# Two more seven-product pairs in the last product's second half, a seventh buffer for arriving weights, residual rows fetched in halves: one Hymba layer in float32

## The chip, the core and the metric

One core of a Trainium2 chip runs the kernel. The metric is the device time of one execution in microseconds. The kernel before was timed in three runs: 1082.09 us in the median, 1081.95 at the lowest, 1083.99 at the highest.

## The reference, cut to what matters

256 tokens with 2048 features pass one layer. All arrays are float32.

```
u    = rmsnorm(h, ln1_w)
proj = u @ W_in                      # six pieces of 1024 columns
y    = [RG-LRU group | retention group]   # 2048 columns
h    = h + y @ w_out                 # 2048 x 2048
u    = rmsnorm(h, ln2_w)
ff   = silu(u @ w_gate) * (u @ w_up) # 5632 columns each
h    = h + ff @ w_down               # 5632 x 2048
out  = rmsnorm(h, final_norm_w)
```

The change lies mostly in `ff @ w_down`, called "down" below, and in buffers that all parts share.

## The kernel before, in words

Each float32 number is cut into a high part (rounded to the format that TensorE multiplies) and the rest, a low part. One product of two blocks then takes three matmuls (`three`: high by high, high by low, low by high). ScalarE makes the high part with a cast and VectorE the low part with a subtraction (`split`, lines 123 and 124; names `wh`, `wl` for a pair of weight blocks, `bh`, `bl` for a single one, `ah`, `al` for a left block, `sh`, `sl` for sums of left blocks).

**Weights.** They arrive in loads of 128 x 1024 numbers (512 KB) from the queue of SyncE (SP) into `raw` buffers, of which there are six, and pass through `split` into `wh` and `wl` buffers, of which there are four pairs. From the fourth multiplication block on (`swap`), two more `raw` buffers (`raw2`) and two more pairs of split buffers (`split2`) exist: every fourth load takes one of the former, every third split one of the latter. Before the last gate/up block, `stop_more` ends their use, and ahead of down `swap_back` gives their memory to the residual rows (`resid2`, eight tiles) and the final norm's weights (`fw`), which GpSimd's queue then loads.

**Pairs.** After the projections every product runs over *pairs*: two 128-row pieces of the left matrix for both token halves (a11, a12, a21, a22) by the four weight blocks of 512 columns that go with them. A plain pair takes eight products. A summed pair takes seven (Strassen-Winograd): VectorE adds up weight blocks (`Quad.add`, line 661, four additions of 128 x 512) and left blocks (s1 to s4), and the sums are split as well. A plain pair needs two wide splits of weights, a summed one a narrow split (b11) and three wide ones.

**Down.** `down_block(d, ...)` runs twice, for d = 0 (output columns 0 to 1023) and d = 1 (1024 to 2047), with 22 pairs each; the texts call them block 0 and block 1. `ORDER_DOWN[d]` lists the order of the pairs, `SUMMED_DOWN[d]` which of them are summed. The left blocks are the same in both (`make_left` keeps them in `dl`). The results p1, p5, p6, p7 of the summed pairs and c11, c12, c21, c22 collect in TensorE's accumulators. When a collected c is complete, VectorE adds it to the residual row tile `htok` (line 941), ScalarE squares that tile for the final norm into a tile called `junk` that nobody reads (line 979, with a running sum), and VectorE multiplies `htok` by the norm's weights `fw` (line 984). For block 0 this work falls into the start of block 1.

**Small tiles.** Everything of 128 x 512 (left blocks, `bh`, `bl`, `part`, `junk`, `sq`) comes from one rotating pool of 60 buffers (`act_tile`). A new tile waits for the last reader of the tile that had its buffer before.

**The start.** `squares` (line 308) squares the eight tiles of x for the first norm. The first square goes to `sumsq`, the other seven to `sq` tiles that GpSimd adds to `sumsq` (lines 310, 311); TensorE then sums over partitions (`rms`, line 271) among the matmuls of the next projection.

A scheduler of the framework decides each engine's order when the kernel is built; the two last pairs of block 1 alone have a fixed order. Every engine works through its own list strictly in that order.

## Time and profile before

| | |
|---|---|
| median of three runs | 1082.09 us (1081.95 to 1083.99) |
| profiled execution | 1082.46 us |
| its span in the trace | 1080.7 us |
| outside the span | 1.8 us |
| TensorE busy (matmul / weight load) | 1070.2 us (99%) / 897.7 us (83%) |
| VectorE busy | 964.1 us (89%) |
| ScalarE busy | 664.5 us (61%) |
| GpSimd busy | 57.2 us (5%) |
| mean granted TensorE clock | 0.998 |

Busy times are sums over one execution. An engine that is off the chain of waits can be idle at no cost; TensorE, which is on it nearly throughout, can't.

### The profile page before, as it was taken

What the parts mean: (1) busy time and instruction counts of PE and PEld (TensorE: products, weight loads), DVE (VectorE), ACT (ScalarE), POOL (GpSimd) and SP (SyncE); (2) the same over time, 40 slices, a digit from 0 to 9 for tenths busy, and PEclk for the clock granted to TensorE, in tenths of its full rate; (3) what the DMA queues carried; (4) which work ended last, traced back from release to release, by engine and by line L of the source; (5) the groups of instructions that cost most, each with busy time, mean ns of one, the idle gap of its engine ahead of it and who ended that gap; (6) DMA issues with size and microseconds to landing.
All of it is one profiled execution on the core that took longest, in us unless ns stands there. A gap on an engine that the chain in (4) does not pass through costs nothing.

```text
span 1080.7 us, 14590 instructions
## 1 busy us (share of the span) xinstructions
PE 1070.2 (99%) x5089; PEld 897.7 (83%) x5089; DVE 964.1 (89%) x1399; ACT 664.5 (61%) x947; POOL 57.2 (5%) x73
## 2 busy tenths in 40 slices
PE   9999999999999999999999999999999999999997
PEld 7888888888888888888888888888888888888886
DVE  7889789988878889989999999999999889997886
ACT  7666644468756676656656565665656656654563
POOL 0602230000000000000000000000002000000001
PEclk9999999999999999999999999999999999999999
DMA  9965475554556588677776777777767856474662
GB/s 325 336 213 171 159 254 166 183 176 158 192 195 234 183 304 273 231 235 256 257 270 228 251 260 242 263 269 232 258 234 270 289 181 214 162 245 159 214 212 101
DMA packets 71386, 244.62 MB, mean 226 GB/s; under 512 B 8208, under 2 KB 8592, under 8 KB 71312
## 3 DMA queue, kind: packets, MB, share of 16 engines
q1 hardware_dynamic: 68400, 236.34, 64.6%
q0 software_dynamic: 1472, 4.72, 1.3%
q10 hardware_dynamic: 1440, 2.62, 0.6%
q8 instruction: 40, 0.66, 0.2%
q14 instruction: 34, 0.28, 0.1%
HBM read 239.46 MB, written 4.19 MB: 225 GB/s over the span
## 4 chain that ended last, share of the span: by engine, by line
PE 98%; DVE 1%; DMA 1%; POOL 0%; SPq 0%; ACT 0%; issue 0%; POOLq 0%; ACTq 0%
PE c L685 22%; PE c L683 22%; PE c L684 22%; PE fm L194 11%; PE fm L196 5%; PE tm L174 3%; PE tm L175 3%; PE tm L176 3%; PE p L683 1%; PE p L685 1%; PE p L684 1%; PE ft L865 1%; DMA x<-in_x 1%; PE ht L588 0%; PE sc L492 0%; DVE wl L124 0%
## 5 line engine op out<-in xcount | busy, mean ns | idle before, releaser
L123 ACT CAST wh<-raw 128x1024 fp32r<-128x1024 f32 (+1 forms) x498 | 462.9, 959 | 323.8 <-PE c L685 130.8
L124 DVE TENSOR_TENSOR wl<-raw,wh 128x1024 fp32r<-128x1024 f32 (+1 forms) x498 | 542.2, 1115 | 72.5 <-ACT wh L123 71.2
L684 PE MATMUL c<-wl,ah 128*128 128x512 f32 x826 | 322.7, 391 | 0.0
L685 PE MATMUL c<-wh,al 128*128 128x512 f32 x826 | 321.8, 390 | 0.0
L683 PE MATMUL c<-wh,ah 128*128 128x512 f32 x826 | 280.3, 391 | 0.0
L683 PEld LDWEIGHTS c<-wh,ah 128*128 128x128 f32 x826 | 155.1, 188 | 32.0 <-ACT wh L123 0.3
L685 PEld LDWEIGHTS c<-wh,al 128*128 128x128 f32 x826 | 155.2, 188 | 31.8
L684 PEld LDWEIGHTS c<-wl,ah 128*128 128x128 f32 x826 | 155.2, 188 | 31.6
L194 PE MATMUL fm<-u,wh 128*128 128x512 f32 x512 | 161.4, 396 | 0.0
L196 PEld LDWEIGHTS fm<-u,wl 128*128 128x128 f32 x512 | 96.1, 188 | 22.4
L196 PE MATMUL fm<-u,wl 128*128 128x256 f32 x512 | 101.2, 279 | 0.0
L661 DVE TENSOR_TENSOR raw<-raw,raw 128x512 f32<-128x512 f32 x114 | 78.4, 689 | 2.0
L661 DVE TENSOR_TENSOR raw<-raw 128x512 f32<-128x512 f32 x114 | 78.3, 688 | 1.4
L194 PEld LDWEIGHTS fm<-u,wh 128*128 128x128 f32 x512 | 78.4, 189 | 0.3
L684 PE MATMUL c<-wl,sh 128*128 128x512 f32 x192 | 74.3, 390 | 0.0
L685 PE MATMUL c<-wh,sl 128*128 128x512 f32 x192 | 73.7, 390 | 0.0
L683 PE MATMUL c<-wh,sh 128*128 128x512 f32 x192 | 67.3, 391 | 0.3 <-ACT sh L123 0.3
L176 PE MATMUL tm<-wh,u 128*128 128x512 f32 x128 | 48.7, 391 | 0.0
L175 PE MATMUL tm<-wl,u 128*128 128x512 f32 x128 | 48.7, 393 | 0.0
L174 PE MATMUL tm<-wh,u 128*128 128x512 f32 x128 | 46.9, 394 | 1.4 <-ACT u L298 1.4
L683 PEld LDWEIGHTS c<-wh,sh 128*128 128x128 f32 x192 | 36.1, 188 | 8.1 <-ACT sh L123 0.7
L685 PEld LDWEIGHTS c<-wh,sl 128*128 128x128 f32 x192 | 36.1, 188 | 7.5
(247 smaller groups left out, 1027.4 us busy)
## 6 DMA issues: line engine op xcount, KB each, us to landing
raw<-in_w_gu SPq DMA_DIRECT2D x216, 512.0 KB, 5.3
raw<-in_w_down SPq DMA_DIRECT2D x91, 512.0 KB, 4.6
raw<-in_w_out SPq DMA_DIRECT2D x34, 512.0 KB, 3.7
raw<-in_w_lx SPq DMA_DIRECT2D x16, 512.0 KB, 6.4
raw<-in_w_k SPq DMA_DIRECT2D x16, 512.0 KB, 3.6
raw<-in_w_q SPq DMA_DIRECT2D x16, 512.0 KB, 4.2
raw<-in_w_rg SPq DMA_DIRECT2D x16, 512.0 KB, 3.5
raw<-in_w_lg SPq DMA_DIRECT2D x16, 512.0 KB, 3.5
```

Of the source, the lines that this page charges most:

```text
L123: act.copy(out=dst_h, in_=src)
L124: v.tensor_tensor(out=dst_l, in0=src, in1=dst_h.bitcast(F32), op=ALU.subtract)
L174: pe.matmul(ps, ah, wh, start=first, stop=False)
L175: pe.matmul(ps, ah, wl, start=False, stop=False)
L176: pe.matmul(ps, al, wh, start=False, stop=last)
L194: pe.matmul(ps, wh, hl, start=n + i == 0, stop=False)
L196: pe.matmul(ps[:, :S], wl, hl[:, :S], start=False, stop=n + i == len(order) - 1)
L661: v.tensor_tensor(out=dst, in0=a, in1=b, op=ALU.add)
L683: pe.matmul(p, ah, bh, start=first, stop=False, skip_group_check=onto)
L684: pe.matmul(p, ah, bl, start=False, stop=False, skip_group_check=onto)
L685: pe.matmul(p, al, bh, start=False, stop=last, skip_group_check=onto)
L865: pe.transpose(pt[:, o : o + P], g[:, (2 * b + c) * P : (2 * b + c) * P + P], ident)
```

## The change

- Block 1 of down has nine summed pairs instead of seven: 12 and 19 are added. They were summed in block 0 already, so their left sums exist; the tiles of these sums now come from a pool of their own (`sums`, four buffers) that is opened in block 0 and closed after the pair in place 7 of block 1. The order of block 1 changes so that plain and summed pairs alternate from its second pair on, with 12 and 19 in front.
- There are seven `raw` buffers all through. The extra `raw2` buffers are taken by kind: by the loads of `Direct` and by the second half of a block's last plain pair. The extra split buffers stay in use until the pair in place 6 of block 0 of down.
- The residual rows come back in two halves: four tiles, then `fw`, from the pair in place 9 of block 0 on, and the other four tiles after the pair in place 7 of block 1.
- `sumsq` and the rotation tables `cr`, `sr` come from the pool of 60 instead of buffers of their own.

```diff
-SUMMED_DOWN = (9, 12, 15, 17, 19), (5, 7, 9, 11, 13, 15, 17)
-ORDER_DOWN = (3, 4, 0, 5, 6, 1, 7, 8, 2) + tuple(range(9, 22)), tuple(range(22))
+SUMMED_DOWN = (9, 12, 15, 17, 19), (5, 7, 9, 11, 12, 13, 15, 17, 19)
+ORDER_DOWN = (3, 4, 0, 5, 6, 1, 7, 8, 2) + tuple(range(9, 22)), (0, 12, 1, 19, 2, 5, 3, 7, 4, 9, 6, 11, 8, 13, 10, 15, 14, 17, 16, 18, 20, 21)
+BESIDE = (12, 19)
...
-    rpool = ctx.enter_context(tc.tile_pool(name="raw", bufs=6))
+    rpool = ctx.enter_context(tc.tile_pool(name="raw", bufs=7))
...
-    def raw_tile():
-        turn_of[0] += 1
-        pool_ = more[0] if more and turn_of[0] % 4 == 0 else rpool
+    def raw_tile(brief=False):
+        pool_ = more[0] if more and brief else rpool
...
-    sumsq = cpool.tile([P, 512], F32, name="sumsq")
+    sumsq = act_tile("sumsq")
...
-    cr = cpool.tile([P, S], F32, name="cr")
-    sr = cpool.tile([P, S], F32, name="sr")
+    turned = act_tile("turned")
+    cr, sr = turned[:, :S], turned[:, S:]
...
+            if i in hooks[ordered]:
+                program.append(([], hooks[ordered][i]))
...
+            place = sum_tile if p in BESIDE else act_tile
+            dl[p] = Left(ff[p], p in EARLY_DOWN + SUMMED_DOWN[0] + SUMMED_DOWN[1], place)
...
+    def rows_back(d):
+        resid[0] = ctx.enter_context(tc.tile_pool(name=f"resid_{d}", bufs=4))
+        for key in [(cb, t) for cb in (2 * d, 2 * d + 1) for t in range(2)]:
+            htok[key] = res_tile("htok")
+            pool.dma_start(out=htok[key], in_=kept[key])
+
     def swap_back():
         extra.close()
+        rows_back(0)
         late.append(ctx.enter_context(tc.tile_pool(name="late", bufs=4)))
-        resid[0] = ctx.enter_context(tc.tile_pool(name="resid2", bufs=8))
-        for key in [(cb, t) for cb in range(4) for t in range(2)]:
-            htok[key] = res_tile("htok")
-            pool.dma_start(out=htok[key], in_=kept[key])
         load_fw()
+        sums_kept.append(beside.enter_context(tc.tile_pool(name="sums", bufs=4)))
+
+    def sums_end():
+        beside.close()
+        rows_back(1)
+
+    hooks = {0: {6: stop_more, 9: swap_back}, 1: {7: sums_end}}
...
-        if b.index == NB + 1:
-            program.append(([], stop_more))
         b.put(after)
-    program.append(([], swap_back))
```

What it does to each engine's list shows in rows of the program, in an engine's order, without times. Numbers at the end of names tell tiles apart; in brackets stands whose progress a row waits for ("DMAHW", "DMASW": a load).

**ScalarE, where block 0 of down ends and block 1 begins, before.** The four squares are the rows of line 979.

```order
L123 CAST wh_1962_9171<-raw_1961_9169 128x1024 [waits DMAHW3_49,DVE_49,PE_49]
L123 CAST wh_1969_9237<-raw_1968_9235 128x1024 [waits DMAHW4_49,DVE_49,PE_49]
L979 ACTIVATE junk_1964_9188,ssq_121<-htok_1735_8244 128x512 [waits DVE_49]
L979 ACTIVATE junk_1965_9203,ssq_121<-htok_1737_8248 128x512 [waits DVE_49,Activation_49]
L979 ACTIVATE junk_1966_9218,ssq_121<-htok_1736_8246 128x512 [waits DVE_49,Activation_49]
L123 CAST wh_1972_9243<-raw_1971_9241 128x1024 [waits DMAHW5_49,PE_49]
L123 CAST wh_1979_9277<-raw_1978_9275 128x1024 [waits DMAHW6_49,PE_49]
L979 ACTIVATE junk_1967_9233,ssq_121<-htok_1738_8250 128x512 [waits DVE_49]
L123 CAST wh_1982_9283<-raw_1981_9281 128x1024 [waits DMAHW7_49,PE_49]
L123 CAST wh_1985_9313<-raw_1984_9311 128x1024 [waits DMAHW0_49,PE_49]
```

All four squares wait for VectorE (or for ScalarE's own earlier rows), none for TensorE; the casts of weights around them wait for loads and for TensorE to have read the buffer's last content.

**ScalarE at the same place, with the change** (`wh_1957` is the second half of block 1's first pair; `bh_1960`, `wh_1967`, `wh_1969`, `wh_1971` belong to its second pair, 12; `bh_1984` to its fourth, 19).

```order
L123 CAST wh_1957_9159<-raw_1956_9157 128x1024 [waits DMAHW2_49,DVE_49,PE_49]
L123 CAST bh_1960_9165<-raw_1959_9163 128x512 [waits DMAHW3_49,DVE_49]
L123 CAST wh_1967_9231<-raw_1966_9229 128x1024 [waits DMAHW4_49,PE_49,Activation_49]
L983 ACTIVATE junk_1962_9182,ssq_120<-htok_1826_8628 128x512 [waits DVE_49,PE_49]
L123 CAST wh_1969_9239<-raw_1959_9163 128x1024 [waits DVE_49,Activation_49]
L983 ACTIVATE junk_1963_9197,ssq_120<-htok_1828_8632 128x512 [waits PE_49]
L983 ACTIVATE junk_1964_9212,ssq_120<-htok_1827_8630 128x512 [waits Activation_49]
L983 ACTIVATE junk_1965_9227,ssq_120<-htok_1829_8634 128x512 [waits PE_49]
L123 CAST bh_1984_9289<-raw_1983_9287 128x512 [waits DMAHW7_49,PE_49]
L123 CAST wh_1971_9243<-raw_1966_9229 128x1024 [waits DVE_49]
L123 CAST wh_1974_9249<-raw_1973_9247 128x1024 [waits DMAHW5_49]
```

Three of the four squares now wait for TensorE too; the cast `wh_1969` stands between the first and the second, and `bh_1984`, `wh_1971` and `wh_1974` stand behind the fourth.

**VectorE at the same place, before** (additions of line 941, multiplications of line 984, splits of line 124).

```order
L941 TENSOR_TENSOR htok_1735_8244<-c11_1663_7914,htok_1735_8244 128x512 [waits PE_49]
L124 TENSOR_TENSOR wl_1963_9172<-raw_1961_9169,wh_1962_9171 128x1024 [waits DMAHW3_49,Activation_49]
L941 TENSOR_TENSOR htok_1737_8248<-c12_1666_7926,htok_1737_8248 128x512 [waits PE_49]
L941 TENSOR_TENSOR htok_1736_8246<-c21_1665_7922,htok_1736_8246 128x512 [waits DVE_49,PE_49]
L920 TENSOR_TENSOR htok_1738_8250<-htok_1738_8250,part_1951_9145 128x512 [waits DMASW7_49,DVE_49]
L124 TENSOR_TENSOR wl_1970_9238<-raw_1968_9235,wh_1969_9237 128x1024 [waits DMAHW4_49,Activation_49]
L984 TENSOR_TENSOR htok_1735_8244<-htok_1735_8244,fw_1743_8260 128x512 [waits DMASW0_49,Activation_49]
L984 TENSOR_TENSOR htok_1737_8248<-htok_1737_8248,fw_1744_8262 128x512 [waits DMASW1_49,Activation_49]
```

**VectorE there with the change** (945 and 988 are the same lines as 941 and 984, moved down by four).

```order
L945 TENSOR_TENSOR htok_1829_8634<-c22_1666_7917,htok_1829_8634 128x512 [waits PE_49]
L661 TENSOR_TENSOR raw_1959_9163<-raw_1959_9163 128x512 [waits DVE_49]
L661 TENSOR_TENSOR raw_1959_9163<-raw_1959_9163,raw_1966_9229 128x512 [waits DVE_49]
L661 TENSOR_TENSOR raw_1966_9229<-raw_1959_9163,raw_1966_9229 128x512 [waits DVE_49]
L988 TENSOR_TENSOR htok_1826_8628<-htok_1826_8628,fw_1830_8639 128x512 [waits DMASW4_49,Activation_49]
L661 TENSOR_TENSOR raw_1966_9229<-raw_1966_9229 128x512 [waits DVE_49]
L124 TENSOR_TENSOR wl_1970_9240<-raw_1959_9163,wh_1969_9239 128x1024 [waits Activation_49]
L988 TENSOR_TENSOR htok_1828_8632<-htok_1828_8632,fw_1831_8641 128x512 [waits DMASW5_49,Activation_49]
L988 TENSOR_TENSOR htok_1827_8630<-htok_1827_8630,fw_1830_8639 128x512 [waits Activation_49]
L988 TENSOR_TENSOR htok_1829_8634<-htok_1829_8634,fw_1831_8641 128x512 [waits Activation_49]
L124 TENSOR_TENSOR bl_1985_9290<-raw_1983_9287,bh_1984_9289 128x512 [waits DMAHW7_49,Activation_49]
L124 TENSOR_TENSOR wl_1972_9244<-raw_1966_9229,wh_1971_9243 128x1024 [waits Activation_49]
```

A multiplication by `fw`, which needs the first square, now stands ahead of the last weight addition of pair 12 and of the split `wl_1970` behind it; three more stand ahead of the splits `bl_1985` and `wl_1972`.

**TensorE at the start of block 1, with the change, first piece:** the last readers of the first pair's left tiles, the 22nd to 26th matmul of block 1.

```order
L683 MATMUL c21_1979_9265<-wh_1957_9159,ah_1638_7794 128x512
L684 MATMUL c21_1979_9265<-wl_1958_9160,ah_1638_7794 128x512
L685 MATMUL c21_1979_9265<-wh_1957_9159,al_1639_7795 128x512
L683 MATMUL p1_1986_9293<-bh_1960_9165,ah_1838_8658 128x512 [waits DVE_49,Activation_49]
L683 MATMUL c11_1976_9253<-wh_1967_9231,ah_1838_8658 128x512 [waits Activation_49]
```

The 23rd is the last reader of `ah_1638`, the 24th that of `al_1639`.

**TensorE there, second piece:** the 32nd to 38th matmul.

```order
L684 MATMUL p1_1986_9293<-bl_1961_9166,ah_1838_8658 128x512 [waits DVE_49]
L685 MATMUL p1_1986_9293<-bh_1960_9165,al_1839_8659 128x512
L683 MATMUL p5_1987_9303<-wh_1969_9239,sh_1841_8667 128x512 [waits Activation_49]
L684 MATMUL p5_1987_9303<-wl_1970_9240,sh_1841_8667 128x512 [waits DVE_49]
L685 MATMUL p5_1987_9303<-wh_1969_9239,sl_1842_8668 128x512
L683 MATMUL p1_1986_9293<-bh_1984_9289,ah_1918_9004 128x512 [waits Activation_49]
L683 MATMUL p6_1988_9307<-wh_1971_9243,sh_1841_8667 128x512 [waits Activation_49]
```

The 34th, 35th, 37th and 38th matmul are the first to read `wh_1969`, `wl_1970`, `bh_1984` and `wh_1971`.

**TensorE in the first projection, at the first norm's sum over partitions, before.**

```order
L194 MATMUL fm_94_526<-u_38_263,wh_82_470 128x512
L196 MATMUL fm_94_526<-u_37_258,wl_83_471 128x256
L196 MATMUL fm_94_526<-u_38_263,wl_83_471 128x256
L194 MATMUL fm_94_526<-u_42_298,wh_82_470 128x512
L271 MATMUL rms_95_543<-ones_92,sumsq_111 128x2 [waits Pool_49]
L271 MATMUL rms_95_543<-ones_92,sumsq_111 128x2
```

**The same with the change.**

```order
L194 MATMUL fm_96_525<-u_40_262,wh_84_469 128x512
L196 MATMUL fm_96_525<-u_39_257,wl_85_470 128x256
L196 MATMUL fm_96_525<-u_40_262,wl_85_470 128x256
L271 MATMUL rms_97_542<-ones_92,sumsq_2_111 128x2 [waits Pool_49]
L271 MATMUL rms_97_542<-ones_92,sumsq_2_111 128x2
L194 MATMUL fm_96_525<-u_44_297,wh_84_469 128x512
```

The two `rms` matmuls stand one matmul of 512 columns earlier; on ScalarE the first square, which stood among the casts of the first weights, now follows the two copies of line 1040 (1036 before) and precedes the other seven squares.

## Rows read from the trace of the kernel before

**Rows 1.** The page: span, busy times, the engines of the chain.

```profile
span 1080.7 us, 14590 instructions
...
PE 1070.2 (99%) x5089; PEld 897.7 (83%) x5089; DVE 964.1 (89%) x1399; ACT 664.5 (61%) x947; POOL 57.2 (5%) x73
...
PE 98%; DVE 1%; DMA 1%; POOL 0%; SPq 0%; ACT 0%; issue 0%; POOLq 0%; ACTq 0%
```

**Rows 2.** Busy time by stretch (columns in the second line).

```profile
core 0: us, PE busy (x) PEld busy (x) DVE busy (x) ACT busy (x) POOL busy (x), PEclk, DMA share, GB/s
0.00:10.00 10.00, 7.54 (x32) 6.28 (x33) 4.11 (x17) 5.82 (x12) 0.34 (x6) 1.00 0.67 217
10.00:360.00 350.00, 350.00 (x1856) 300.65 (x1855) 304.21 (x515) 221.09 (x354) 46.30 (x50) 1.00 0.62 212
360.00:380.00 20.00, 19.70 (x87) 15.82 (x86) 18.66 (x29) 13.56 (x19) 0.00 (x0) 1.00 0.61 199
380.00:955.00 575.00, 575.00 (x2590) 476.87 (x2589) 536.58 (x707) 360.30 (x477) 6.39 (x12) 1.00 0.73 247
955.00:1055.00 100.00, 100.00 (x443) 82.87 (x442) 83.96 (x97) 54.30 (x65) 0.00 (x0) 1.00 0.60 199
1055.00:1080.70 25.70, 17.97 (x91) 15.17 (x89) 16.60 (x39) 9.47 (x22) 4.16 (x5) 0.92 0.26 92
```

**Rows 3.** The chain of waits, 961 to 964 us: start, us, what.

```profile
961.96 0.91 PE c L683 x4
```

**Rows 4.** Groups by form, 955 to 1060 us, VectorE and ScalarE.

```profile
L124 DVE TENSOR_TENSOR wl<-raw,wh 128x1024 fp32r<-128x1024 f32 x46 | 54.9, 1220 | 7.1 <-ACT wh L123 7.1
L661 DVE TENSOR_TENSOR raw<-raw 128x512 f32<-128x512 f32 x14 | 9.6, 688 | 0.2
...
L124 DVE TENSOR_TENSOR bl<-raw,bh 128x512 fp32r<-128x512 f32 x11 | 7.3, 690 | 8.9 <-ACT bh L123 8.9
```

**Rows 5.** Timeline of ScalarE, 957 to 965 us: start, us, what, idle before.

```profile
958.37 1.06 ACT L123 CAST wh<-raw 128x1024 fp32r<-128x1024 f32 x1 [1.44 <-PE c L685]
959.33 0.62 ACT L979 ACTIVATE junk<-htok 128x512 f32<-128x512 f32 x1
...
960.08 0.63 ACT L979 ACTIVATE junk<-htok 128x512 f32<-128x512 f32 x1
```

**Rows 6.** Timeline of VectorE, 953 to 968 us.

```profile
961.97 1.29 DVE L984 TENSOR_TENSOR htok<-htok,fw 128x512 f32<-128x512 f32 x2
...
964.44 2.36 DVE L124 TENSOR_TENSOR wl<-raw,wh 128x1024 fp32r<-128x1024 f32 x2
```

**Rows 7.** Timeline of ScalarE, 985 to 1035 us.

```profile
1005.80 0.62 ACT L123 CAST bh<-raw 128x512 fp32r<-128x512 f32 x1 [3.31 <-DMA raw<-in_w_down]
1006.33 3.92 ACT L123 CAST wh<-raw 128x1024 fp32r<-128x1024 f32 x4
...
1016.27 0.62 ACT L123 CAST bh<-raw 128x512 fp32r<-128x512 f32 x1 [4.21 <-DMA raw<-in_w_down]
```

**Rows 8.** Timelines of ScalarE, GpSimd and TensorE's weight loads, 27 to 46 us.

```profile
29.74 3.76 ACT L308 ACTIVATE sq<-x 128x512 f32<-128x512 f32 x7
...
30.47 12.58 POOL L310 TENSOR_TENSOR sumsq<-sumsq,sq 128x512 f32<-128x512 f32 x7 [29.59 <-ACT sq L308]
43.13 1.60 POOL L311 TENSOR_TENSOR sumsq<-sumsq 128x256 f32<-128x256 f32 x1
...
44.85 0.64 PEld L271 LDWEIGHTS rms<-ones,sumsq 128*128 128x128 f32 x4
```

**Rows 9.** Single loads issued at 999.3 and 1001.6 us: last column us to landing.

```profile
raw<-in_w_down SPq DMA_DIRECT2D x1, 512.0 KB, 3.2
raw<-in_w_down SPq DMA_DIRECT2D x1, 512.0 KB, 5.5
```

**Rows 10.** Timelines of ScalarE and TensorE, 906 to 911 us.

```profile
906.96 1.05 ACT L123 CAST wh<-raw 128x1024 fp32r<-128x1024 f32 x1 [1.37 <-PE c L685]
...
909.66 1.07 PE L683 MATMUL c<-wh,ah 128*128 128x512 f32 x4
```

More of the change, by code (lines that the diff above doesn't have):

```diff
@@ L56, in tile_hymba_layer @@
     tpool = early.enter_context(tc.tile_pool(name="tmp", bufs=6))
-    late, resid, more, turn_of = [], [xpool], [], [0, 0]
+    late, resid, more, turn_of = [], [xpool], [], [0]
     extra = ExitStack()
@@ L74, in split_tiles @@
     def split_tiles():
-        turn_of[1] += 1
-        pool_ = more[1] if more and turn_of[1] % 3 == 0 else wpool
+        turn_of[0] += 1
+        pool_ = more[1] if more and turn_of[0] % 3 == 0 else wpool
         return [pool_.tile([P, 1024], F32R, tag=g, name=nm(g)) for g in ("wh", "wl")]
-    def raw_tile():
-        turn_of[0] += 1
-        pool_ = more[0] if more and turn_of[0] % 4 == 0 else rpool
+    def raw_tile(brief=False):
+        pool_ = more[0] if more and brief else rpool
         return pool_.tile([P, 1024], F32, tag="raw", name=nm("raw"))
@@ L552, in tile_hymba_layer, with __init__ @@
         names = ("a11", "a21", "a12", "a22", "s1", "s2", "s3", "s4")
-        def __init__(self, f, sums):
+        def __init__(self, f, sums, place=act_tile):
             self.h, self.l = [act_tile("ah", F32R)], [act_tile("al", F32R)]
@@ L564, in __init__ @@
                 v.tensor_tensor(out=s4, in0=a12, in1=s2, op=ALU.subtract)
-                self.h.append(act_tile("sh", F32R))
-                self.l.append(act_tile("sl", F32R))
+                self.h.append(place("sh", F32R))
+                self.l.append(place("sl", F32R))
                 split(self.h[1], self.l[1], g)
@@ L625, in __init__ @@
             self.parts = {}
-            self.apart = False
+            self.apart = self.brief = False
         def cut(self, names, raw):
@@ L639, in load @@
         def load(self, half):
-            r = raw_tile()
+            r = raw_tile(self.brief and half == 1)
             nc.sync.dma_start(out=r, in_=self.src[:, half * 1024 : half * 1024 + 1024])
@@ L769, in load @@
         def load(self, half):
-            r = raw_tile()
+            r = raw_tile(True)
             nc.sync.dma_start(out=r, in_=self.src[:, 1024:2048])
@@ L837, in put @@
                     quad = Quad(self.src(i), False)
+                    quad.brief = n == 0
                     run = lambda i=i, quad=quad, k=k, n=n: self.plain(i, quad, k == 0, n == 0)
@@ L904, in make_left @@
         if dl[p] is None:
-            dl[p] = Left(ff[p], p in EARLY_DOWN + SUMMED_DOWN[0] + SUMMED_DOWN[1])
+            place = sum_tile if p in BESIDE else act_tile
+            dl[p] = Left(ff[p], p in EARLY_DOWN + SUMMED_DOWN[0] + SUMMED_DOWN[1], place)
     def down_block(d, ahead):
@@ L1104, in stop_more, with sum_tile @@
         more.clear()
+    beside, sums_kept = ExitStack(), []
+    def sum_tile(name, dt):
+        return sums_kept[0].tile([P, 512], dt, tag="sum", name=nm(name))
+    def rows_back(d):
[3 more added lines that the diff above has]
+            pool.dma_start(out=htok[key], in_=kept[key])
     def swap_back():
         extra.close()
+        rows_back(0)
         late.append(ctx.enter_context(tc.tile_pool(name="late", bufs=4)))
-        resid[0] = ctx.enter_context(tc.tile_pool(name="resid2", bufs=8))
-        for key in [(cb, t) for cb in range(4) for t in range(2)]:
-            htok[key] = res_tile("htok")
-            pool.dma_start(out=htok[key], in_=kept[key])
         load_fw()
+        sums_kept.append(beside.enter_context(tc.tile_pool(name="sums", bufs=4)))
[3 more added lines that the diff above has]
+    hooks = {0: {6: stop_more, 9: swap_back}, 1: {7: sums_end}}
     blocks = [Block(d, lambda i, d=d: A["w_out"][8 * d + i], y, out_post(d), STEPS[d], SUMMED[d]) for d in range(2)]
```

## The prediction

> **What bounds the kernel now.** I read the page first [rows 1]: TensorE is busy 99% of the span and is 98% of the chain of waits. The share alone does not say whether a saved matmul shortens the run; the busy time by stretch does [rows 2]. From 10 to 360 us and from 380 to 1055 us TensorE has not one hundredth of a microsecond without a matmul. All its idle time is 2.46 us in the first 10 us, 0.30 us between 360 and 380 us, and 7.73 us behind 1055 us, where the output is finished. So every matmul taken out is worth its full spacing, and every new wait of TensorE costs its full length: nothing else lies beside it. In block 1 of down, 955 to 1055 us, VectorE works 83.96 of 100 us and ScalarE 54.30: both are ahead of TensorE, by an amount that a changed order can use up.
>
> **What the change removes.** Two pairs go from eight products to seven, at three matmuls each: six matmuls of 512 columns. Four in a row take 0.91 us [rows 3], 0.2275 each, so **-1.36 us**. That is the whole gain on TensorE.
>
> **What it adds to VectorE.** A summed pair needs four additions of line 661, one narrow split and one wide split more than a plain one [rows 4]. Rows follow each other faster than they last: two additions of this size in 1.29 us at 0.69 each start 0.60 apart, two wide splits in 2.36 us at 1.22 each 1.14 apart [rows 6]; the narrow split, 0.69 us long like the addition [rows 4], is put at 0.60. So 4 x 0.60 + 0.60 + 1.14 = 4.14 us a pair, 8.3 us for two. One plain and one summed pair together are 15 x 3 x 0.2275 = 10.24 us of TensorE and 2 x 1.14 + 4 x 0.60 + 0.60 + 3 x 1.14 = 8.70 us of VectorE. On the mean it still has 1.5 us to spare in each such period, so I put this work at nothing; the cover is gone where a load comes more than 1.5 us late (rival two).
>
> **The start of block 1.** Here the rows of the program's order decide. Block 0's four squares have no new work, but they now take buffers in the pool of small tiles whose last readers belong to block 1's first matmuls: by the counts on which the compiled rows wait, the first square waits for the 23rd matmul of block 1 (last reader of `ah_1638`), the second for the 24th, the fourth for the 32nd, and `bh_1984` for the 33rd. Behind them on ScalarE stand casts that TensorE needs at once, and on VectorE a multiplication by `fw` that needs the first square stands ahead of an addition and a split. I count from the start of block 1's first matmul: the n-th starts at (n-1) x 0.2275, and is over 0.39 after that (four of them, 0.91 apart as a group, end after 1.07 [rows 10]). On ScalarE a square with its accumulator takes 0.75 us (959.33 to 960.08), a wide cast 0.96 (958.37 to 959.33) [rows 5], a narrow one 0.53 (1005.80 to 1006.33) [rows 7].
> - The 23rd matmul ends at 5.40. First square to 6.15, `wh_1969` to 7.11; the 34th matmul needs that at 7.51, in time.
> - VectorE: multiplication 6.15 to 6.75, addition to 7.35, `wl_1970` to 8.49. The 35th matmul wants it at 7.74: wait 0.75.
> - ScalarE: squares to 7.86, 8.61 and 9.36, `bh_1984` to 9.89. The 37th matmul, at 8.19 and 0.75 late, is ready at 8.94: wait 0.95.
> - `wh_1971` to 10.85. The 38th is ready at 8.42 + 1.70 = 10.12: wait 0.73.
> - Next late would be the 45th with `wh_1974`, cast by 11.81 and wanted at 10.01 + 2.43 = 12.44: in time. The waits end there.
>
> Sum **+2.4 us**. Before, the squares wait for no matmul and follow a cast at once, at 959.33 and 960.08 [rows 5]. Bounds: 0, if TensorE comes to this place with the squares already done, which the counts exclude unless I misread them; 3.4, if the pairs' loads come late besides, by what is left of the 2.3 us below. I take the worked value.
>
> **The first norm.** `sumsq` used to be squared while ScalarE waited for loads; now it is squared behind the copies, ahead of seven squares that take 3.76 us, 0.53 each [rows 8]. GpSimd's chain of additions, from 30.47 us to 44.73 (43.13 + 1.60), starts 0.53 later and ends at 45.26. TensorE loaded the sum at 44.85, 0.12 behind it, without waiting; now the sum can be loaded at 45.38 at the latest, and the matmul's place is one matmul earlier, at 44.62. Between 0.4 (no lag, load partly hidden) and 0.76 us; I take **+0.6**. Cover that hides it, there is none: the next matmuls stand behind it.
>
> **Block 0 of down.** Its pairs keep their order, but the splits' extra buffers go at place 6 and the loads' order shifts. Pair 12 there gets its first weights from the third load of a bunch. A load alone lands in 3.2 us, one that follows others in 5.5 [rows 9]: 2.3 us more. TensorE had some 1.65 us in hand at its tightest there in before (a cast started at 906.96 and 1.05 long, its matmul at 909.66 [rows 10]). So 0, if the load is alone, to 1.6, if it is late and the lead is smaller by 1 us; nearest the case of the row, with 2.3 - 1.65 = 0.65 us left over at worst as things stood. I take **+0.4**.
>
> [...]
>
> The residual rows in halves and `fw` travel on GpSimd's queue, tens of microseconds ahead of their use; the tables `cr`, `sr` and the seventh buffer by itself touch no row that TensorE waits for. Nothing for them. The last forty rows of every engine are the same as before, so the 7.73 us at the end stay.
>
> **Sum.** -1.36 + 2.4 + 0.6 + 0.4 = **+2.0 us**. On the profiled execution (1082.46 us, of it 1080.7 in the span and 1.8 around it) that is 1084.5; this execution is 0.4 above the median of 1082.09, so the forecast for the median is **1084.1 us**. A difference of under 0.2%, 2.16 us, can't be told from none: 1079.93 to 1084.25 counts as the same.
>
> **Rivals.**
> - *One: the waits don't come.* If ScalarE and VectorE run further ahead than I count (the seventh buffer lets loads start sooner), only the matmuls remain, with or without the norm's 0.6: 1080.7 to 1081.3 us. For it: VectorE had 16 us idle in 100 there [rows 2]. Against: the order of the squares is fixed, whatever the loads do.
> - *Two, slower: the alternating part can't feed TensorE.* In before ScalarE waits 3.31 and 4.21 us for the load of a summed pair's first block [rows 7]. With nine periods in a row, a load at 5.5 instead of 3.2 us [rows 9] is 2.3 late against 1.5 to spare: 0.8 a period. It decides from about 4.7 us of landing time on. Nine periods give 7 us, half of them 3.6; on top of the forecast 1087 to 1091, middle 1088. Against: with seven buffers this load should be first in its bunch.
> - *Three, slower: VectorE as the bound of block 1.* If its 8.3 us found no room, 1082.1 - 1.4 + 8.3 = 1089.0. Against: 16 us of room.
> - *Four: faster beyond doubt.* That takes 2.16 us; 1.36 and the 0.30 between 360 and 380 us don't reach it, so 0.5 of the 2.46 in the first 10 us would have to go as well, through the additional buffer: 1079.5. Against: the loads of x at the start keep their order.
>
> By the Trainium skill, page "Perfetto Trace Analysis", section "Identifying the Most-Contended Engine", the engine with the highest occupancy is the one to look at, and TensorE is judged by its weight loads instead of its matmuls. That makes VectorE, 89% against 83%, the bound, and rival three the outcome. The trace disagrees: TensorE's matmuls follow each other without a gap where VectorE idles.
>
> **Chances.** Forecast 0.61 (own range 1083.0 to 1085.6), rival one 0.19, two and three together 0.15, four 0.05. The forecast lies at the border: 0.33 of it within 0.2%, 0.28 slower. Same: 0.33 + 0.17 = 0.50; slower: 0.28 + 0.15 = 0.43; faster: 0.05 + 0.02 of rival one = 0.07. The range runs from rival one, 1080.9, to the forecast with its upper bounds (1.0 at the start of block 1, 1.2 in block 0, 0.2 at the norm, half a period's lateness), 1087.0.
>
> **What would show it.** Right: TensorE 0 idle in 380 to 955 us but near pair 12, then three gaps of 0.7 to 1 us within 4 us, each released by `wl_1970`, `bh_1984` or `wh_1971`, and one of 0.6 at 45 us. Wrong: no gap behind block 1's 34th matmul (rival one), or a gap in each period of 10 us released by `bh` (rival two) or by VectorE's splits without waiting for loads (rival three). What breaks the forecast soonest is the landing time of loads in bunches, which the new order changes and no row of before shows for it.

## The result, and the profile after

The changed kernel takes 1085.16 us (median of 13 runs, 1083.62 to 1085.71), the kernel before on the same chip 1082.93 (13 runs, 1081.80 to 1083.99): a ratio of 1.0022, 95% interval 1.0015 to 1.0030. That is 2.2 us slower between the medians, at the border of the 0.2% that a measurement tells from no change. The profiled execution took 1085.53 us, 3.07 more than the one of before.

The page of the kernel after, the lines that answer to [rows 1]:

```profile
span 1083.7 us, 14591 instructions
...
PE 1072.3 (99%) x5083; PEld 897.5 (83%) x5083; DVE 972.0 (90%) x1411; ACT 666.9 (62%) x951; POOL 56.5 (5%) x73
...
PE 94%; POOL 1%; DMA 1%; DVE 1%; issue 1%; ACT 1%; SPq 0%; POOLq 0%; ACTq 0%
```

TensorE has six matmuls fewer and yet is busy 2.1 us longer. Its share of the chain fell from 98 to 94%. Most of that is the stretch before 45 us, where the chain now runs back over GpSimd's sum, rows of VectorE and two loads instead of TensorE; the time that was lost shows better by stretch. Busy time, kernel after (columns as in [rows 2]):

```profile
30.00:50.00 20.00, 19.91 (x116) 17.34 (x115) 15.04 (x16) 14.66 (x22) 15.42 (x10) 1.00 0.96 360
...
960.00:975.00 15.00, 13.66 (x51) 10.26 (x50) 13.87 (x20) 8.82 (x16) 0.00 (x0) 0.89 0.32 100
975.00:1055.00 80.00, 80.00 (x355) 66.26 (x354) 69.62 (x79) 44.93 (x49) 2.12 (x4) 1.00 0.65 218
```

One stretch of 15 us has the new idle time, 1.34 us. From 975 to 1055 us, where the other seven seven-product pairs run, TensorE has none. In the 15 us the granted clock is 0.89 besides. The same view in steps of 2 us:

```profile
966.00:968.00 2.00, 1.11 (x4) 0.48 (x3) 2.00 (x4) 2.00 (x6) 0.00 (x0) 1.00 0.13 29
968.00:970.00 2.00, 1.55 (x5) 1.08 (x5) 2.00 (x4) 2.00 (x3) 0.00 (x0) 0.73 0.62 234
970.00:972.00 2.00, 2.00 (x6) 1.52 (x5) 2.00 (x3) 1.53 (x2) 0.00 (x0) 0.50 0.24 78
972.00:975.00 3.00, 3.00 (x14) 2.48 (x13) 3.00 (x5) 0.91 (x2) 0.00 (x0) 0.94 0.95 269
```

First come the gaps, 966 to 970 us, with VectorE and ScalarE busy without a pause. Then, behind them, TensorE is busy all the time at half of its clock (0.50 of 2.4 GHz, its level of 1.2): 6 matmuls in 2 us. Busy time alone would have called that stretch full.

The timeline of TensorE, kernel after, at the gaps (start, us, what, idle before and releaser):

```profile
965.69 0.39 PE L683 MATMUL p<-wh,sh 128*128 128x512 f32 x1
966.86 0.50 PE L684 MATMUL p<-wl,sh 128*128 128x512 f32 x1 [0.79 <-DVE wl L124]
967.20 0.40 PE L685 MATMUL p<-wh,sl 128*128 128x512 f32 x1
967.70 0.50 PE L683 MATMUL p<-bh,ah 128*128 128x512 f32 x1
968.65 0.57 PE L683 MATMUL p<-wh,sh 128*128 128x512 f32 x1 [0.45 <-ACT wh L123]
```

Idle time understates a wait, since a matmul's end lies 0.39 us behind its start and the next may start 0.2275 after it. So I read the distances of the starts; what a distance has over 0.2275 is called lost by starts below. That is 0.95 us at `wl` (965.69 to 966.86), 0.11 behind it, 0.27 at `bh` and 0.72 at `wh`: 2.05 us at the three places that the prediction named. Behind that come 0.14 and seven starts 0.43 apart, at half clock: with what is left until the clock is back, some 1.6 us. By starts the stretch loses 3.8 us in all.

The chain of causes stands on ScalarE. Its timeline in the kernel after:

```profile
963.62 0.63 ACT L983 ACTIVATE junk<-htok 128x512 f32<-128x512 f32 x1 [6.16 <-PE c L684]
...
964.25 1.04 ACT L123 CAST wh<-raw 128x1024 fp32r<-128x1024 f32 x1
965.20 0.62 ACT L983 ACTIVATE junk<-htok 128x512 f32<-128x512 f32 x1
...
967.04 0.60 ACT L123 CAST bh<-raw 128x512 fp32r<-128x512 f32 x1
967.55 2.94 ACT L123 CAST wh<-raw 128x1024 fp32r<-128x1024 f32 x3
```

A square of a residual row, whose result `junk` nobody reads, waits 6.16 us for a matmul of block 1. In before it followed a cast at once [rows 5]. Behind it stand casts of pairs 12 and 19. On VectorE, same kernel:

```profile
964.38 0.69 DVE L988 TENSOR_TENSOR htok<-htok,fw 128x512 f32<-128x512 f32 x1 [1.06 <-ACT junk L983]
964.99 0.69 DVE L661 TENSOR_TENSOR raw<-raw 128x512 f32<-128x512 f32 x1
965.59 1.22 DVE L124 TENSOR_TENSOR wl<-raw,wh 128x1024 fp32r<-128x1024 f32 x1
966.73 1.89 DVE L988 TENSOR_TENSOR htok<-htok,fw 128x512 f32<-128x512 f32 x3
968.54 0.68 DVE L124 TENSOR_TENSOR bl<-raw,bh 128x512 fp32r<-128x512 f32 x1
```

VectorE idled 1.06 us in front of the first multiplication, and the split that TensorE wanted at 965.92 (965.69 + 0.2275) stands two rows behind it and ends at 966.81.

The first norm, weight loads of TensorE in the kernel after:

```profile
45.08 0.52 PEld L271 LDWEIGHTS rms<-ones,sumsq 128*128 128x128 f32 x4 [0.28 <-POOL sumsq L311]
```

A wait of 0.28 us stands where there was none [rows 8], and from there on TensorE is 0.29 us behind the kernel before.

The last matmul starts 2.92 us later than in before: -1.36 of the matmuls, 0.29 of the norm, 0.20 near 853 us (a weight load waits 0.33 us for VectorE's low half `al`, foreseen by no step) and 3.79 at the start of block 1, about 2.2 of it waits and 1.6 clock.

### The profile page after: what moved, and what is told of

Its sections match the earlier page's. It is cut to its first block, busy times and chain, and to the rows that moved or that the text cites. A ratio compares the mean times of both kernels' runs of the same rounds, so it can differ in the third digit from the quotient of the medians.

```text
span 1083.7 us, 14591 instructions
## 1 busy us (share of the span) xinstructions
PE 1072.3 (99%) x5083; PEld 897.5 (83%) x5083; DVE 972.0 (90%) x1411; ACT 666.9 (62%) x951; POOL 56.5 (5%) x73
## 3 DMA queue, kind: packets, MB, share of 16 engines
HBM read 239.46 MB, written 4.19 MB: 225 GB/s over the span
## 4 chain that ended last, share of the span: by engine, by line
PE 94%; POOL 1%; DMA 1%; DVE 1%; issue 1%; ACT 1%; SPq 0%; POOLq 0%; ACTq 0%
PE c L683 22%; PE c L685 22%; PE c L684 22%; PE fm L194 10%; PE fm L196 5%; PE tm L174 2%; PE tm L176 2%; PE tm L175 2%; PE p L685 1%; PE p L684 1%; PE p L683 1%; POOL sumsq L310 1%; PE ft L868 1%; DMA raw<-in_w_lx 1%; DMA raw<-in_w_v 0%
## 5 line engine op out<-in xcount | busy, mean ns | idle before, releaser
L684 PE MATMUL c<-wl,ah 128*128 128x512 f32 x814 | 317.7, 390 | 0.0
L685 PE MATMUL c<-wh,al 128*128 128x512 f32 x814 | 314.9, 389 | 0.0
L683 PE MATMUL c<-wh,ah 128*128 128x512 f32 x814 | 276.8, 392 | 0.0
L685 PEld LDWEIGHTS c<-wh,al 128*128 128x128 f32 x814 | 152.8, 188 | 31.7 <-DVE al L124 0.3
L684 PEld LDWEIGHTS c<-wl,ah 128*128 128x128 f32 x814 | 152.9, 188 | 31.3
L661 DVE TENSOR_TENSOR raw<-raw,raw 128x512 f32<-128x512 f32 x118 | 81.1, 688 | 2.0
L661 DVE TENSOR_TENSOR raw<-raw 128x512 f32<-128x512 f32 x118 | 80.6, 686 | 1.1
L1119 POOL DMA_DIRECT2D htok<-kept_rows x8 | 4.3, 546 | 796.4 <-DVE wl L124 704.0
```

Of the source, the lines that this page charges most:

```text
L661: v.tensor_tensor(out=dst, in0=a, in1=b, op=ALU.add)
L683: pe.matmul(p, ah, bh, start=first, stop=False, skip_group_check=onto)
L684: pe.matmul(p, ah, bl, start=False, stop=False, skip_group_check=onto)
L685: pe.matmul(p, al, bh, start=False, stop=last, skip_group_check=onto)
```

## The experiments

**The theories.** *The squares:* three waits at the start of block 1, caused by squares of block 0 which wait for buffers, cost what the six matmuls save and more. *The buffers:* the seventh buffer, the buffers by kind and the halves change when loads land, whatever the pairs are. *The norm:* its wait is a part of the price that can be mended by itself. Seven kernels were timed against the kernel before in two groups, each group on a chip of its own, with medians of before of 1083.17 (27 runs; e1 to e4) and 1083.38 (15 runs; e5 to e7); e8 ran once. The changed kernel was not timed again in these groups, so a comparison with it goes by how far each kernel lies from before in its own series: +2.2 us for the changed one.

Why do the squares wait? Small tiles of 128x512 come from one pool of 60 which goes round. From the code, 44 are held by the high and low halves of the 22 lefts and 14 by the sums of the seven summed pairs that don't take theirs from a pool of their own: 58. Two are free, and pair 12's `bh` and `bl` take them. `junk` can have a buffer only when a left's last matmul has run. In before a plain pair, 1, stood at this place, which takes no small tiles. The experiments move this shortage or remove it.

**e1, the order shifted.** Pair 12 comes one place later, so that the squares are issued ahead of it; 9 and 11, both summed, become neighbours.

```diff
-ORDER_DOWN = ..., (0, 12, 1, 19, 2, 5, 3, 7, 4, 9, 6, 11, 8, 13, ...)
+ORDER_DOWN = ..., (0, 1, 12, 2, 19, 3, 5, 4, 7, 6, 9, 11, 8, 13, ...)
```

> The changed kernel with block 1's order alone altered: 0, 1, 12, 2, 19, 3, 5, 4, 7, 6, 9, 11, 8, 13, ... as before. Pair 12 is third instead of second and 19 fifth, so two plain pairs have given their left tiles back before the weights of 12 ask for small tiles; still nine summed pairs. Small-tile theory (the first squares of block 0's rows wait because the pool of 60 has two free buffers when block 1 starts): the squares wait for no matmul, the three gaps of TensorE at the start of block 1 (2.05 us) go and with them the stretch at half clock behind them (1.7 us): 3.7 us less than the changed kernel, 1081.5, up to 1082.5 if the two summed pairs 9 and 11, now side by side, are late. Rival (VectorE and ScalarE can't carry a ninth summed pair beside block 0's output rows, wherever it stands): the gaps move some microseconds back and the time stays at 1084 to 1085.5.

Measured: 1085.17 us (11 runs, 1083.66 to 1086.84), ratio 1.0019, interval 1.0010 to 1.0028; some 3 us over the expectation of the small-tile theory and inside the range of the rival. Stretches of e1:

```profile
960.00:975.00 15.00, 15.00 (x67) 12.20 (x66) 13.83 (x20) 8.74 (x16) 0.00 (x0) 1.00 0.34 108
975.00:1055.00 80.00, 78.49 (x344) 63.76 (x343) 71.18 (x81) 44.45 (x49) 2.12 (x4) 1.00 0.67 223
```

The start of block 1 is free of waits, as the theory of the squares has it. But TensorE idles 1.51 us further on, at pair 11, and loses 2.6 us there and behind it by starts. TensorE, ScalarE and VectorE of e1 there:

```profile
1021.01 0.50 PE L683 MATMUL p<-wh,sh 128*128 128x512 f32 x1 [1.29 <-ACT wh L123]
...
1012.40 0.62 ACT L123 CAST bh<-raw 128x512 fp32r<-128x512 f32 x1 [4.32 <-DMA raw<-in_w_down]
...
1019.92 5.02 ACT L123 CAST wh<-raw 128x1024 fp32r<-128x1024 f32 x5 [4.05 <-DVE raw L661]
```

ScalarE waits 4.32 us for the first load of the next summed pair, 13 by the count of the narrow casts. In VectorE's list that pair's narrow split and its first two additions stand ahead of pair 11's last two additions (1018.40 and 1019.11), so VectorE idles 1.62 us (before 1013.05), then works without a pause from 1013 to 1019.8 us, and ScalarE waits 4.05 us for its additions. That two summed pairs stand side by side here may add to this, but it is not shown to be the cause: e2, where summed and plain pairs alternate, loses time at the same pair with the same waits.

**e2, the pairs of before.** Pairs, sums and order of block 1 as before, with all the buffers, halves and loads of the change.

```diff
-SUMMED_DOWN = (9, 12, 15, 17, 19), (5, 7, 9, 11, 12, 13, 15, 17, 19)
+SUMMED_DOWN = (9, 12, 15, 17, 19), (5, 7, 9, 11, 13, 15, 17)
-ORDER_DOWN = ..., (0, 12, 1, 19, 2, 5, ...)
+ORDER_DOWN = ..., tuple(range(22))
```

> The changed kernel with block 1's seven summed pairs and their plain order 0 to 21 put back; the seventh buffer, the extra ones by kind, the rows in halves, the first norm's square and the sums' own pool stay. Small-tile theory and the rival that blames the ninth pair: no gaps at the start of block 1, six matmuls more: 1085.2 - 3.7 + 1.4 = 1082.9. Rival that blames the buffers or the rows in halves: the gaps stay, 1085 to 1086.5.

Measured: 1085.06 us (11 runs, 1083.80 to 1086.29), ratio 1.0018, interval 1.0010 to 1.0027. The number is that of the theory of the buffers, the place is not: the gaps did not stay where they were. Stretches, TensorE, ScalarE and VectorE of e2:

```profile
960.00:975.00 15.00, 15.00 (x67) 12.42 (x67) 12.10 (x15) 8.00 (x15) 0.00 (x0) 1.00 0.72 237
975.00:1055.00 80.00, 78.77 (x345) 64.13 (x344) 63.35 (x71) 41.90 (x46) 0.00 (x0) 1.00 0.56 185
...
1021.30 0.50 PE L683 MATMUL p<-wh,sh 128*128 128x512 f32 x1 [1.01 <-ACT wh L123]
1021.64 0.39 PE L683 MATMUL c<-wh,ah 128*128 128x512 f32 x1
1022.26 0.97 PE L683 MATMUL c<-wh,ah 128*128 128x512 f32 x3 [0.22 <-ACT wh L123]
...
1013.50 0.62 ACT L123 CAST bh<-raw 128x512 fp32r<-128x512 f32 x1 [4.30 <-DMA raw<-in_w_down]
...
1020.21 3.90 ACT L123 CAST wh<-raw 128x1024 fp32r<-128x1024 f32 x4 [4.19 <-DVE raw L661]
...
1014.15 0.69 DVE L124 TENSOR_TENSOR bl<-raw,bh 128x512 fp32r<-128x512 f32 x1 [3.52 <-ACT bh L123]
```

There is no wait at the start of block 1, so that one does come with the pairs. In its place some 1.8 us are lost near 1021 us (starts 1.40 apart before 1021.30 and 0.62 before 1022.26, where 0.2275 is due), at pair 11. The loads for this place are the DMA issues of e2 from 1008 to 1012 us:

```profile
raw<-in_w_down SPq DMA_DIRECT2D x3, 512.0 KB, 7.3
```

The three loads of one bunch land after 7.3 us in the median, and ScalarE waits 4.30 us for pair 13's first load there. VectorE idles 3.52 us for that pair's narrow split, ahead of pair 11's last two additions, and ScalarE waits 4.19 us for those. This is rival two's mechanism, in a kernel in which it was not expected. Whether the seventh buffer, the buffers by kind or the halves make the bunch was not tried apart; e8, which has none of them, loses 1.0 us in the same part of block 1.

**e3, the first square early.** The square into `sumsq` is issued behind the second `make_u` instead of behind the copies.

```diff
+    def first_square():
+        act.activation(out=sumsq, in_=xt[0], func=AF.Square)
...
-            sq = act_tile("sq") if i else sumsq
-            act.activation(out=sq, in_=xt[i], func=AF.Square)
             if i:
+                sq = act_tile("sq")
+                act.activation(out=sq, in_=xt[i], func=AF.Square)
...
+    def made_u(k):
+        make_u(k)
+        if k == 1:
+            first_square()
```

> The changed kernel with the first square of x issued where ScalarE was idle before, right behind the second piece of u. My reading of the first norm: the sum over partitions is reached in time again, the 0.3 us at 45 us goes, 1084.9. Rival: the wait at 45 us came from the matmul's earlier place alone; then nothing changes, 1085.2.

Measured: 1084.74 us (11 runs, 1083.93 to 1085.22), ratio 1.0012, interval 1.0003 to 1.0021. Weight loads of TensorE at the norm, and a stretch at the start of block 1, both of e3:

```profile
44.47 0.52 PEld L271 LDWEIGHTS rms<-ones,sumsq 128*128 128x128 f32 x4 [0.46 <-POOL sumsq L314]
...
970.00:972.00 2.00, 2.00 (x10) 1.64 (x9) 2.00 (x3) 1.56 (x2) 0.00 (x0) 1.00 0.21 57
```

The norm's matmul moved up by four places together with its operand, and the wait stayed. The edit did not remove what it was to remove, and says nothing of the norm's price. It shows another thing: the gaps at the start of block 1 are those of the kernel after (distances of 1.18, 0.49 and 0.95 us), but this profile has no half clock behind them: 10 matmuls from 970 to 972 us. It loses 0.8 us elsewhere instead, near 980 and 1042 us. The clock's fall is no fixed part of the gaps' price.

**e4, squares without a buffer.** Block 0's four squares write their unread result over the accumulator in PSUM that has just been read.

```diff
-                    down_post(cb, t, 0, 512)
+                    down_post(cb, t, 0, 512, junk=None if d else ps[c])
...
-        j = act_tile("junk")
+        j = junk if junk is not None else act_tile("junk")
```

> The changed kernel with block 0's four squares written over the accumulator that their row was just added from, so that they need no small tile. If the squares as such are the cause, the gaps go: 1081.5. Small-tile theory: the two free buffers are then asked for by pair 19's bh, which waits for the 24th and later matmul of block 1 and stands ahead of two casts of pair 12; the wait moves there, 1 to 2.6 us of gaps remain and some of the half clock: 1083 to 1085.

Measured: 1089.60 us (5 runs, 1087.81 to 1090.23), ratio 1.0059, interval 1.0047 to 1.0072: over 4 us more than either outcome that was expected. ScalarE and VectorE of e4:

```profile
960.61 0.60 ACT L983 ACTIVATE c<-htok 128x512 f32<-128x512 f32 x1 [0.48 <-DVE htok L945]
...
962.93 0.62 ACT L123 CAST bh<-raw 128x512 fp32r<-128x512 f32 x1 [1.59 <-PE c L684]
964.27 1.05 ACT L123 CAST wh<-raw 128x1024 fp32r<-128x1024 f32 x1 [0.72 <-DVE raw L661]
967.82 3.89 ACT L123 CAST wh<-raw 128x1024 fp32r<-128x1024 f32 x4 [2.49 <-DVE raw L661]
...
960.49 1.28 DVE L988 TENSOR_TENSOR htok<-htok,fw 128x512 f32<-128x512 f32 x2
...
962.29 1.29 DVE L988 TENSOR_TENSOR htok<-htok,fw 128x512 f32<-128x512 f32 x2
```

The squares are done by 961.2 us and wait for no matmul. The next tile that wants a buffer is now `bh` of pair 19, and it waits 1.59 us for a matmul in their place. So two small tiles are missing, whoever asks first. But this wait is not what holds TensorE up in e4: VectorE works without a pause from 959.3 to 968.3 us, with four multiplications by `fw` ahead of three of pair 12's additions, and ScalarE's casts wait for VectorE's additions (0.72 and 2.49 us). TensorE idled 2.12 us from 960 to 975 and 3.03 from 975 to 1055 us; the second loss begins where ScalarE waits 5.86 us for a load (985.91), and why that load is late is open. The theory of the squares fell here in its first form: with them out of the way, VectorE's order holds TensorE up by as much.

**e5, room for two tiles.** The two narrow halves `bh` and `bl` of pair 12 in block 1 come from the pool of the sums, which gets six buffers instead of four; the room comes from `fw`, whose second half is fetched later, when the pool of the sums is closed.

```diff
-        late.append(ctx.enter_context(tc.tile_pool(name="late", bufs=4)))
-        load_fw()
-        sums_kept.append(beside.enter_context(tc.tile_pool(name="sums", bufs=4)))
+        late.append(ctx.enter_context(tc.tile_pool(name="late", bufs=2)))
+        load_fw(0)
+        sums_kept.append(beside.enter_context(tc.tile_pool(name="sums", bufs=6)))
...
+            if d and i == 12:
+                quads[-1].place = sum_tile
...
+        late[0] = ctx.enter_context(tc.tile_pool(name="late_1", bufs=2))
+        load_fw(1)
```

> The changed kernel, all nine pairs in their order, with two more small tiles where block 1 starts: the first split block of pair 12 (bh and bl) comes from the sums' pool, made six instead of four, and to pay for it the final norm's weights for the second half are fetched only when that pool closes. No square of block 0's rows waits for a matmul any more. Small-tile theory: the gaps behind the 34th matmul of block 1 go but for up to 0.7 us at the 38th, no half clock behind them: 1.4 to 2.05 us for the gaps and some 1.0 us for the clock, which fell in 8 of 13 runs, less than the changed kernel: 1082.1 to 1082.8. Rival (VectorE and ScalarE are late there for their work, whoever owns the tiles): gaps of 2 us stay, 1085. Second rival (gaps only move: the alternating part is on the edge, and what is not lost at the start is lost later): gaps near 1020 us, 1084 to 1085.

Measured: 1082.51 us (11 runs, 1081.96 to 1083.08), ratio 0.9990, interval 0.9981 to 0.9999, as expected. Stretches, TensorE and ScalarE of e5:

```profile
960.00:975.00 15.00, 14.41 (x63) 11.40 (x62) 15.00 (x20) 7.74 (x13) 0.00 (x0) 1.00 0.40 132
975.00:1055.00 80.00, 80.00 (x355) 66.15 (x354) 70.35 (x80) 46.78 (x53) 3.17 (x6) 1.00 0.67 225
...
967.04 0.74 PE L684 MATMUL p<-wh,sh 128*128 128x512 f32 x2 [0.57 <-ACT wh L123]
...
959.59 0.63 ACT L986 ACTIVATE junk<-htok 128x512 f32<-128x512 f32 x1
...
960.60 0.63 ACT L986 ACTIVATE junk<-htok 128x512 f32<-128x512 f32 x1 [0.29 <-DVE htok L946]
```

The squares follow VectorE's additions as in before, and one gap of 0.6 us of idle time is left (1.0 us by starts), behind which the clock stays at 1.00. VectorE is busy 15.00 of the 15 us, so this last gap is put down to it and not to the buffers. Against before, e5 is 0.9 us faster and the changed kernel 2.2 slower; the intervals of the two ratios don't touch, so the edit is worth some 3 us. By its own interval e5 is faster than before by 0.1 to 2.1 us, which is less than the 0.2% asked for a sure difference. Its profiled execution does not show that gain: behind the first 10 us it is 0.3 us later than the one of before (-1.36 of the matmuls, 0.29 at the norm, 0.23 near 853 us and 1.16 at the start of block 1). The gain in the median would have to come from executions of before that were longer than the profiled one (1082.46 us, against a median of 1083.38 in this series); none of them was traced.

**e6, six arriving buffers.** The seventh buffer of the pool `raw` is taken back.

```diff
-    rpool = ctx.enter_context(tc.tile_pool(name="raw", bufs=7))
+    rpool = ctx.enter_context(tc.tile_pool(name="raw", bufs=6))
```

> The changed kernel with six buffers for arriving weights instead of seven, the rest as it is. If the seventh buffer had no part in the gaps at the start of block 1, they stay (2 us and some of the clock). If it carries the alternation, loads come later and there are more gaps in block 0 and block 1: 1086 to 1090. If the seventh buffer is what hurts (loads in bunches of three), fewer gaps: 1083.

Measured: 1088.48 us (4 runs, 1088.14 to 1089.24), ratio 1.0044, interval 1.0031 to 1.0058: 5.1 us over before, where the changed kernel was 2.2 over. The gaps at the start of block 1 are still there (starts 1.10, 1.13 and 0.97 us apart), and others come in the alternating part. TensorE of e6:

```profile
993.24 0.50 PE L683 MATMUL p<-bh,ah 128*128 128x512 f32 x1 [2.04 <-ACT bh L123]
```

That `bh` waited 7.15 us for its load (ScalarE, 992.57). So the buffer is needed by the new order and does not cause the first waits; this is rival two's mechanism again, and in the changed kernel the seventh buffer holds it off.

**e7, six arriving buffers and 62 small ones.** The two missing tiles are given to the common pool, in the room of the seventh buffer.

```diff
-    apool = ctx.enter_context(tc.tile_pool(name="acts", bufs=60))
-    rpool = ctx.enter_context(tc.tile_pool(name="raw", bufs=7))
+    apool = ctx.enter_context(tc.tile_pool(name="acts", bufs=62))
+    rpool = ctx.enter_context(tc.tile_pool(name="raw", bufs=6))
```

> As the one before, with the memory of the seventh buffer given to two more small tiles (62). Small-tile theory: against the kernel with six and 60, no square waits for a matmul and the gaps around the 34th to 38th matmul of block 1 shrink to at most 1 us, while gaps from late loads stay: 1 to 3 us less than with 60. Rival (work, not tiles): no difference between the two.

Measured: 1088.80 us (4 runs, 1088.13 to 1089.27), ratio 1.0046, interval 1.0032 to 1.0060; no gain over e6, so the expectation fell. ScalarE and VectorE of e7, and a stretch:

```profile
962.16 0.63 ACT L983 ACTIVATE junk<-htok 128x512 f32<-128x512 f32 x1 [0.48 <-DVE htok L945]
...
968.71 1.99 ACT L123 CAST wh<-raw 128x1024 fp32r<-128x1024 f32 x2 [3.69 <-DVE raw L661]
...
963.79 1.28 DVE L988 TENSOR_TENSOR htok<-htok,fw 128x512 f32<-128x512 f32 x2
...
970.00:972.00 2.00, 2.00 (x5) 1.61 (x6) 2.00 (x2) 1.69 (x3) 0.00 (x0) 0.50 0.05 4
```

The squares are free, but early squares bring the multiplications by `fw` early too (from 961.98 us on), four of them ahead of two of pair 12's additions, and ScalarE waits 3.69 us for VectorE's additions. In e5 the first two of pair 12's additions start at 953.36 and 955.70 us, in e7 at 960.78 and 963.19; so in e5 VectorE has half of them behind it when the multiplications come. Between the two stand the seventh buffer, the place of the two tiles and the later fetch of half of `fw`; which of them lets the additions start sooner was not tried apart. So two more tiles alone, with six arriving buffers, did not close the gap: TensorE waits 2.00 us from start to start in front of `wh` (967.81 to 969.81).

**e8, before with the moved tiles alone.** The kernel before, with only `sumsq` and the two tables in the pool of small tiles.

```diff
-    sumsq = cpool.tile([P, 512], F32, name="sumsq")
+    sumsq = act_tile("sumsq")
...
-    cr = cpool.tile([P, S], F32, name="cr")
-    sr = cpool.tile([P, S], F32, name="sr")
+    turned = act_tile("turned")
+    cr, sr = turned[:, :S], turned[:, S:]
```

> The kernel before with only the first norm's part of the change: sumsq and the rotation tables from the pool of small tiles. I expect a gap of 0.1 to 0.4 us at the sum over partitions near 45 us and no other difference; the 2 us at the start of block 1 don't come. One look, for the trace.

Measured, in a single run: 1082.98 us, 0.4 under the median of before beside it. Weight loads of TensorE and ScalarE in e8:

```profile
44.19 0.52 PEld L271 LDWEIGHTS rms<-ones,sumsq 128*128 128x128 f32 x4 [0.28 <-POOL sumsq L311]
...
1016.95 0.62 ACT L123 CAST bh<-raw 128x512 fp32r<-128x512 f32 x1 [4.96 <-DMA raw<-in_w_down]
```

The wait of 0.28 us is that of the kernel after, and [rows 8] have none: the moved tiles alone make it. But "no other difference" did not hold. From 995 us on e8 loses 1.0 us by starts, most of it at 999.4 and 1020.2 us, and ScalarE waits 4.96 us for pair 13's first load, where it waited 4.21 in before [rows 7]. So with the pairs and the arriving buffers of before, block 1 already stands at the edge here. Whether the moved tiles bring this about, or the loads of this one execution, a single run can't tell.

## Why the prediction was right, point by point

The forecast of 1084.1 us lies 1.1 under the median of 1085.16; against before's median in the same series it said +2.0 and +2.2 was measured. The side and the main cause were right. That the size came out so near is partly luck: what it added at +3.4 measured 2.7 in the profiled execution, and a term that was not foreseen, 1.6 us of clock, made up for it there.

- *Six matmuls, -1.36 us:* TensorE shows six fewer, and outside the start of block 1 no new loss by starts but 0.29 at 45 us and 0.20 near 853 us. No run has this term by itself: e5 still has 1.7 us of losses in its profiled execution.
- *The waits at the start of block 1, +2.4:* right in place, number, cause and releasers. Worked out were 0.75, 0.95 and 0.73; measured 0.95, 0.27 (0.38 with the 0.11 ahead of it) and 0.72, together 2.05. The second was over-sized: ScalarE's squares and their accumulators took 0.61 to 0.62 each where I took 0.75 (965.20, 965.82 and 966.43 to 967.04). That two small tiles are short, whoever asks first, I had not seen; `bh` in e4 and the free squares in e5 show it. That the tiles are the whole cause is not shown: with the squares free, VectorE's order of additions and multiplications still costs some 2.5 us by starts in e4 and in e7, and e5 has both the tiles and earlier additions.
- *The first norm, +0.6:* 0.29. The mechanism was right (e8); the delay was over-sized. The squares on ScalarE began 0.20 us sooner than in before (29.54 against 29.74), which was not reckoned with, so GpSimd's sum ended at 45.03 and not at the 45.26 worked out.
- *Block 0, pair 12, +0.4:* nothing came there. The lead sufficed. This term was wrong, as was the silence on the 0.20 us near 853 us.
- *The new work of VectorE at nothing:* right from 975 us on (80.00 of 80.00 us full), not at the start of block 1, where it is full for 15 us in e5 and makes the last gap there.
- *Rows in halves and `fw` at nothing:* no wait of TensorE in the kernel after is released by them. The seventh buffer, put at nothing as well, is not nothing: without it the new order takes 2.9 us more (e6).
- *Not foreseen, the clock:* half clock behind the gaps, 1.6 us in the profiled execution. This is the missing term of the sum. How much of it is in the median is open. The eight runs with a mean granted clock of 0.996 average 1085.3 us and the five at 0.998 or more 1084.8, so by that it is worth 0.5 us and not 1.6; but this mean takes in the end of the run too, where the clock falls in before as well (0.92 from 1055 us on), so it marks the fall only roughly. Terms without the clock, -1.36 + 2.05 + 0.14 + 0.29 + 0.20 = 1.3 us, stand against 1.9 for the five (1084.8 less 1082.93): 0.6 us are unassigned.

**The rivals.** *One*, no waits, was wrong for the changed kernel; e5 comes nearest to it, with one gap left. *Two* did not come in the kernel after, but e1, e2 and e6 show that it is near: in each ScalarE waits 4.3 us or more for the load of a summed pair's first block and TensorE loses time behind it, and in e8 as well. By its own bounds, 3.6 to 7 us on top of 1084.1, its middle was 1089 and not 1088. *Three*, VectorE as the bound of the whole of block 1, is excluded by the full stretch at 69.62 busy of 80 us. The page "Perfetto Trace Analysis" of the Trainium skill, section "Identifying the Most-Contended Engine", judges TensorE by the share of peak arithmetic that it reaches as well as by its weight loads; the prediction took the weight loads alone, and by those VectorE came first. By this trace VectorE sets the pace for some 10 us, not for the 100. *Four* was not seen.

## What to carry to other kernels

When a pool of buffers that goes round is full, a tile that nobody reads can stop an in-order engine: before reordering, count which tiles live at each place, and whose last reader frees the next one. Taking away the buffer's first claimant (e4) hands the wait to the next one in line, and freed instructions can crowd another engine's list (e4, e7): see what they let loose before counting the gain. Two more buffers, with the load early enough (e5), took most of the gaps away. And a kernel with no gap on its bound engine may yet stand at the edge of one, so that a change which frees that engine shows its other feeders' limits first.

## What the hardware showed that was not expected

- Behind gaps of about 2 us in 3 (966 to 969 us) the granted clock fell to 0.50 for some 3 us in the kernel after (matmuls 0.43 us apart), and again in e7 behind its gaps; in e3, with the same gaps, and in e4 and e6, with about 2.5 us of them by starts in the same place, it stayed at 1.00, and in e5, with one gap of 0.6 us, as well. Why it falls in some executions only, no run here tells.
- Loads of 512 KB that land in 3.2 us alone and 5.5 among others [rows 9] took 7.3 us in the median in a bunch of three (e2).
- The kernel before is less steady than e5: 1082.17 to 1085.80 us in 15 runs, against 1081.96 to 1083.08 in 11 runs of e5 on the same chip. The cause was not tried; loads that come later, as in e8, could make such executions, which no trace of before shows.
